# An attention layer on one core: the identity made on GpSimd, the third token tile's squares shared, eight extra weight buffers, and six changes of order

## The chip, the cores and the metric

The kernel runs on one core of a Trainium2 chip. The metric is the device time of one execution in microseconds, as the median of three runs. The engines are named as in the profile: PE is TensorE (PEld its weight loads), DVE VectorE, ACT ScalarE, POOL GpSimd, SP the engine that issues most DMAs. Each engine works through a list of its own in order, and waits for others through semaphores.

## The reference, cut to what matters

One layer over 512 tokens of width 1024, in float32:

```python
xn   = rms_norm(x, norm_gain)
proj = xn @ w_in                 # q_a k_a v_a g_a | q_i k_i w_i | c_q c_kv k_rope g_b
# group A: an indexer picks, for each query, the 128 best of the keys it may see
score = sum_h w_i[h] * relu(rope(q_i)[h] . rope(k_i)) / sqrt(512)
keys  = top_k(where(admissible, score, -1e30), 128)
o_a   = softmax(rope(norm(q_a)) . rope(norm(k_a))[keys] / 8) @ v_a[keys]
# group B: attention over latents
q_b, (k_nope, v_b) = norm(c_q) @ w_uq, norm(c_kv) @ w_ukv
o_b   = chunk_causal_softmax(norm(q_b) . norm([k_nope, k_rope]) / sqrt(96)) @ v_b
out   = x + concat(o_a * silu(g_a), o_b * silu(g_b)) @ w_out
```

Both groups have eight heads of 64. Query t may read key s if s < (t // 64 + 1) * 64.

## The kernel before, in words

Every operand of a large product is split into a high part, rounded to PE's fast float32 form, and a low part, the difference. A product of two such operands is three matmuls (`mm3`: high by high, high by low, low by high). Weights come in pieces of 128 rows by up to 512 columns: `chunk` loads a piece into a `wst` buffer (DMA issued by SP), ACT copies it to `wh` (the high part), and POOL or DVE subtracts to get `wl` (the low part).

**The opening.** The 512 tokens come as four tiles of 128 (`xin`). For each tile the squares of the first half of the columns are summed on ACT (`SQ`), those of the second half on DVE (`TTR`, a custom instruction that multiplies and sums); for tile 2 ACT takes all 1024 columns (into the buffer `big`). POOL adds the two sums and raises them to the power -0.5 (`POW`), DVE (tile 3: POOL) scales the tile by it (`SCL`), PE transposes it with the help of the identity `ident` (`x_turn`), ACT takes the high part (`XA`) and DVE the low part (`XD`) of each of 16 pieces (two halves of the tokens, eight blocks of columns). Small products with the columns for `k_i`, `w_i` and `k_rope` (`small_step`, high part `SWA`, low part `SWD`) and the products for the indexer's queries (`q_i`) follow. The order of the opening on ACT, DVE and POOL is written out by hand in three calls of `chain`.

**The middle.** `use_qi` turns the indexer's queries by their positions: two multiplications and a sum on DVE, then PE transposes them. `use_small` makes the indexer's key, whose parts are `KIH` (ACT) and `KIL` (DVE). `index` computes scores, and `topk` removes eight maxima at a time from each of three tiles (`MAX8`, `MATCH_REPLACE8`, on DVE, 16 rounds), until 128 are found; then `masks` are made from the scores (L620). Meanwhile PE runs group B's projections and attention and the projections q_a, k_a, v_a (`proj`: in `use`, the sum L905 is the last reader of the PSUM bank for k_a).

**Attention.** For each head h, `qk(h, t)` makes scores of query tile t (PE), adds the mask and takes the row minimum of the negated scores (a custom instruction on DVE, L758), and exponentiates (ACT, L760). `pt(h, b)` transposes the result in three blocks and splits it in parts (`SP[h, b]`: ACT the high part, DVE the low part `pl`, L449). `pv(h, part)` multiplies with the values, adds the two halves (L822), and for every second head multiplies with the gate (L825) and splits the result into `mah` (ACT, L827) and `mal` (L828). In group A the gate and `mal` are POOL's, save for the last pair of heads, which is DVE's. Output products start beside the last heads (`out_part`, the additions to the output `ob` on DVE, L1008).

**What sets the order.** PE's order is that of the code, which weaves several generators by hand. On the other engines a list scheduler of the framework orders the instructions. `after(v, u)` tells it to put v behind u; on one engine that adds no semaphore. `after` is the means of most edits below. Tiles of one tag share a ring of buffers (`BUFS`): a new tile waits for the last use of the one that it replaces. The first eight hardware DMAs go out freely; each later one waits for the landing of the eighth before it.

Of the kernel before, what the change touches and what calls it, by code (L numbers as in the profile page):

```python
# [11 lines left out]
AF = mybir.ActivationFunctionType  # L12
# [76 lines left out]
def layer(ctx: ExitStack, tc: tile.TileContext, x, norm_gain, w_in, a_q_norm, a_k_norm, b_q_latent,  # L89
# [121 lines left out]
    for t in range(NT):  # L211
        nc.sync.dma_start(xin[t // 2][:, t % 2], xv[:, t])
        if t == 1:
            nc.sync.dma_start(ident, cst[:, 768:896])
    for a in range(0, 8, 4):
        ks = slice(a, a + 4)
        nc.sync.dma_start(wst[:, ks, 0:32], wv[:, ks, 3272:3304])
        nc.sync.dma_start(wst[:, ks, 32:104], wv[:, ks, 2560:2632])

    nhalf = P.tile([128, 8], F32, name="nhalf")  # L220
    nc.gpsimd.memset(nhalf, -0.5)
# [67 lines left out]
    def chunk(w, k, c, n, eng, he):  # L289
        st = sb("wst", (128, n))  # L290
        nc.sync.dma_start(st, w[k * 128:(k + 1) * 128, c:c + n])
        h = sb("wh", (128, n), F32R)
        l = sb("wl", (128, n), F32R)
        if he == "A":
            copies.append(nc.scalar.copy(h, st))  # L295
        else:
            E(he).tensor_copy(h, st)
        i = E(eng).tensor_tensor(l, st, f32(h), op=OP.subtract)  # L298
        (subs if eng == "P" else dsubs).append(i)
        return h, l  # L300
# [66 lines left out]
    SQ, TTR, POW, SCL = {}, {}, {}, {}  # L367
    big = sb("qk8", (128, D), name="big")
    for t in range(NT):
        xt = xin[t // 2][:, t % 2]  # L370
        r = small(4)
        if t == 2:
            SQ[t] = nc.scalar.activation(big, xt, AF.Square, scale=D ** -0.5, accum_out=r[:, 0:1])
            other = epsc
        else:
            sq = tmp(), tmp()
            SQ[t] = nc.scalar.activation(sq[0], xt[:, 0:512], AF.Square, scale=D ** -0.5, accum_out=r[:, 0:1])
            TTR[t] = nc.vector.tensor_tensor_reduce(sq[1], xt[:, 512:], xt[:, 512:], 1.0 / D, EPS, OP.mult, OP.add, r[:, 1:2])
            other = r[:, 1:2]
        POW[t] = nc.gpsimd.tensor_tensor(r[:, 2:3], r[:, 0:1], other, op=OP.add), rsqrt(r[:, 3:4], r[:, 2:3])  # L380
        SCL[t] = []
        for xs in (xt[:, 0:512], xt[:, 512:]) if t in (0, 3) else (xt,):
            e = nc.gpsimd if t == 3 else nc.vector
            if t == 3:
                SCL[t].append(e.tensor_scalar(xs, xs, r[:, 3:4], 0.0, op0=OP.mult, op1=OP.add))
            else:
                SCL[t].append(e.tensor_scalar(xs, xs, r[:, 3:4], None, op0=OP.mult))
# [66 lines left out]
    KIL = sb("z3", (128, S), F32R, "kil")  # L454

    def use_small(_, a):
        st = tmp()
        first(nc.scalar.copy(st[:104], a[:104]), KEEP_SMALL)

        def turn():  # L460
# [18 lines left out]
            def turn2():  # L479
                p = psum("tr")  # L480
                for t in range(NT):
                    transpose(p[:, tok(t)], kid[:, t], ident)
                split(KIH, KIL, p)
            later(LAG_KI, turn2)
# [41 lines left out]
    for a in range(0, 8, 4):  # L526
        ks = slice(a, a + 4)
        SWA.append(nc.scalar.copy(SWH[:, ks], wst[:, ks]))
    for k in range(4):
# [8 lines left out]
    for i, ks in enumerate(((0,), (1,), (2, 3), (4, 5), (6, 7))):  # L538
# [3 lines left out]
        if i == 0:  # L542
            xa, xd = [[f[hf, k] for hf in range(2) for k in range(8)] for f in (XA, XD)]
            chain(wake_, SQ[0], SQ[1], SQ[2], gains_, SQ[3], *xa[:2], SWA[0], *xa[2:4], SWA[1], *xa[4:8], copies[0],
                  *xa[8:10], copies[1], *xa[10:12], copies[2], *xa[12:], copies[3], copies[4])
            chain(TTR[0], TTR[1], *SCL[0], *SCL[1], TTR[3], *SCL[2], *xd, dsubs[0], *SWD)
            chain(*POW[0], *POW[1], *POW[2], *POW[3], *SCL[3], *subs[:3])
        if i == 2:
# [15 lines left out]
    def use_qi(t, a):  # L564
# [5 lines left out]
        rope_mul(a3[:, :, 0:32], m, a3[:, :, 0:32], cs32, t, 8, 32)  # L570
        nc.vector.tensor_tensor(q3[:, :, 0:32], a3[:, :, 0:32], m, op=OP.add)

# [20 lines left out]
    def index():  # L593
        for t in (3, 2, 1):
            n = (t + 1) * 128
            acc = masks[t] = ACC[t]
            for h in range(8):
# [11 lines left out]
                yield 1  # L609

    def topk():
        for _ in range(TOPK // 8):
            for t in (3, 2, 1):
                with tc.issue_after(dve[0]):
                    m = sb("m8", (128, 8))
                    nc.vector.max(m, masks[t])  # L616
                    dve[0] = nc.vector.match_replace(masks[t], m, masks[t], -3e38).ins  # L617
                yield 1
# [126 lines left out]
    def attention(heads, turn, score, mask, nq, V, gate, finish):  # L745
# [4 lines left out]
        def qk(h, t):  # L750
# [17 lines left out]
            elif not turn and h > 1 and t == 3:  # L768
                after(m, SP[h - 2, 0][1])
            if not turn and h and t == 0:  # L770
                after(e, SP[h - 1, 0][0])
# [16 lines left out]
        def pt(h, b):  # L788
# [9 lines left out]
            if not turn and b == 2:  # L798
                for v, u in zip(SP[h, 2], SP[h, 0]):
                    after(v, u)  # L800
            PT[h, b] = ph, pl

# [3 lines left out]
        def pv(h, part):  # L806
# [14 lines left out]
            nc.scalar.copy(ov[d], o[s])  # L821
            nc.vector.tensor_tensor(ov[d], o[d], ov[d], op=OP.add)  # L822
            if h % 2:
# [3 lines left out]
                nc.scalar.copy(mh, ov)  # L827
                eng.tensor_tensor(ml, ov, f32(mh), op=OP.subtract)  # L828

# [46 lines left out]

    MB = {}

# [14 lines left out]
    def proj(name, tab):  # L893
        def use(t, a):
# [9 lines left out]
            rsqrt(r[:, 8:16], r[:, 0:8])  # L904
            (nc.gpsimd if name == "q_a" else nc.vector).tensor_tensor(q, c, m, op=OP.add)  # L905
            if name == "q_a":
# [95 lines left out]
    def out_part(name, nk, mh, ml, last=False):  # L1002
        jobs = []

        def job(c, t, a, n):
            def use(t, p):
                o = OB[c][:, t, a:a + n]
                nc.vector.tensor_tensor(o, p[:, :n], o, op=OP.add)  # L1008
                load()
# [41 lines left out]
```

## Time and profile before

| | us |
|---|---|
| median of 3 runs (lowest, highest) | 340.25 (340.21, 340.5) |
| the profiled execution | 339.3 |
| its span, first to last instruction | 337.5 |
| PE busy | 328.1 (97%) |
| DVE busy | 259.0 (77%) |
| ACT busy | 216.2 (64%) |
| POOL busy | 184.5 (55%) |

The span is what the trace covers; 1.8 us of the profiled execution lie outside it. An engine that is busy for nearly all of the span leaves few gaps, and these can be looked at one by one: in a row of the timeline the number in square brackets is the idle time of that engine just before the instruction, and behind the arrow stands what ended it. The ends of matmuls are modelled, and neighbours overlap in the rows, so the distance of two starts tells more about PE than a duration. The granted clock is 1.00 for the whole span.

### The profile page before, as it was taken

The page shows a single profiled execution, that of the slowest core. Times are in us where ns is not written, and L with a number is a line of the kernel's source. Part 1 is how long each engine was busy: PE and PEld are TensorE (multiplying, and loading weights), DVE is VectorE, ACT ScalarE, POOL GpSimd, SP SyncE. Part 2 cuts the span into 40 slices and gives each one's busy share as a digit, 9 for nine tenths or more (in the row PEclk, how much of TensorE's full clock was granted, in tenths as well). Part 3 has the DMA queues.
Part 4 walks back from the last instruction along what each step waited for, and adds up shares of the span by engine and source line. Part 5 has one row for each costly group of instructions (what it writes and reads, how often), then busy time and mean ns, then how long its engine had stood idle before and what let it go on. Part 6 is the DMA issues. An engine that isn't in the chain of part 4 may idle for free.

```text
span 337.5 us, 5484 instructions
## 1 busy us (share of the span) xinstructions
PE 328.1 (97%) x1691; PEld 273.8 (81%) x1691; DVE 259.0 (77%) x627; ACT 216.2 (64%) x531; POOL 184.5 (55%) x201
## 2 busy tenths in 40 slices
PE   7799999999999999999999999999999999999995
PEld 5688788888898988888888888888778788887884
DVE  4753779669999595778898989777997767876466
ACT  4935559583666676878877898434426988977210
POOL 2755553267899996135714579537724544747100
PEclk9999999999999999999999999999999999999999
DMA  7752443233133324014200354208966314420006
GB/s 259 206 163 72 128 119 117 62 102 95 33 103 93 93 72 148 1 34 124 69 27 1 86 139 136 78 0 204 233 157 228 108 55 140 126 63 1 2 0 249
DMA packets 28807, 34.83 MB, mean 103 GB/s; under 512 B 5341, under 2 KB 16874, under 8 KB 28778
## 3 DMA queue, kind: packets, MB, share of 16 engines
q1 hardware_dynamic: 26000, 32.52, 34.2%
q10 hardware_dynamic: 2778, 1.97, 2.1%
q8 instruction: 13, 0.21, 0.2%
q14 instruction: 16, 0.13, 0.1%
HBM read 27.14 MB, written 2.10 MB: 87 GB/s over the span
## 4 chain that ended last, share of the span: by engine, by line
PE 74%; DVE 10%; DMA 5%; issue 4%; ACT 4%; POOL 2%; SPq 1%; DVEq 0%; POOLq 0%
PE mm L130 40%; PE sc L130 11%; PE pv L130 10%; PE tr L134 5%; PE tr L130 5%; DMA wst<-in_w_in 3%; DMA xin<-in_x 2%; DVE ob L1008 2%; PE mm L134 2%; DVE acc L617 1%; DVE z L758 1%; DVE m L616 1%; ACT xh L403 1%; POOL sml L226 1%; POOL wl L298 1%
## 5 line engine op out<-in xcount | busy, mean ns | idle before, releaser
L298 POOL TENSOR_TENSOR wl<-wst,wh 128x512 fp32r<-128x512 f32 (+2 forms) x80 | 100.5, 1266 | 50.8 <-ACT wh L295 46.4
L295 ACT CAST wh<-wst 128x512 fp32r<-128x512 f32 (+2 forms) x89 | 51.1, 585 | 25.9 <-DMA wst<-in_w_in 13.8
L130 PE MATMUL mm<-wh,xh 128*128 128x512 f32 x112 | 47.1, 420 | 0.4 <-DVE tmp L905 0.4
L130 PE MATMUL mm<-wl,xh 128*128 128x512 f32 x112 | 44.5, 397 | 0.0
L130 PE MATMUL mm<-wh,xl 128*128 128x512 f32 x112 | 44.3, 395 | 0.0
L760 ACT ACTIVATE z<-z,sml 128x256 f32<-128x256 f32 (+2 forms) x64 | 35.9, 561 | 10.0 <-DVE sml L758 9.2
L784 POOL TENSOR_SCALAR z<-z,sml 128x512 f32<-128x512 f32 (+2 forms) x32 | 17.9, 560 | 42.1 <-DVE sml L780 31.4
L226 POOL TENSOR_TENSOR sml<-sml,nhalf 128x4 f32<-128x4 f32 (+2 forms) x28 | 32.5, 1163 | 14.9 <-ACT sml L903 13.7
L130 PE MATMUL mm<-xh,wh 128*128 128x512 f32 x88 | 36.7, 417 | 0.0
L130 PE MATMUL mm<-xl,wh 128*128 128x512 f32 x88 | 34.7, 395 | 0.0
L130 PE MATMUL mm<-xh,wl 128*128 128x512 f32 x88 | 34.7, 394 | 0.0
L616 DVE MAX8 m<-acc 128x8 f32<-128x512 f32 (+2 forms) x48 | 26.3, 550 | 0.0
L617 DVE MATCH_REPLACE8 acc<-m,acc 128x512 f32<-128x512 f32 (+2 forms) x48 | 25.9, 540 | 0.0
L130 PEld LDWEIGHTS mm<-wh,xl 128*128 128x128 f32 x112 | 21.1, 188 | 4.8
L130 PEld LDWEIGHTS mm<-wl,xh 128*128 128x128 f32 x112 | 21.2, 189 | 3.5 <-POOL wl L298 0.3
L130 PEld LDWEIGHTS mm<-wh,xh 128*128 128x128 f32 x112 | 21.1, 189 | 3.6 <-issue 0.8
L449 DVE TENSOR_TENSOR pl<-tr,ph 128x512 fp32r<-128x512 f32 (+1 forms) x32 | 17.6, 550 | 5.7 <-ACT ph L449 5.5
L449 ACT CAST ph<-tr 128x512 fp32r<-128x512 f32 (+1 forms) x32 | 15.1, 473 | 9.1 <-PE tr L134 8.8
L758 DVE CUSTOM_DVE_ANT_0 z<-sc,wide,nqb 128x512 f32<-128x512 f32 (+3 forms) x32 | 17.3, 542 | 4.2 <-PE sc L130 4.0
L130 PE MATMUL sc<-kl,bhl 96*128 96x512 f32 (+3 forms) x96 | 20.0, 320 | 0.0
L130 PEld LDWEIGHTS mm<-xh,wl 128*128 128x128 f32 x88 | 16.5, 188 | 4.1
L130 PEld LDWEIGHTS sc<-kl,bhl 96*128 96x128 f32 x96 | 16.6, 189 | 3.0
(248 smaller groups left out, 876.7 us busy)
## 6 DMA issues: line engine op xcount, KB each, us to landing
wst<-in_w_in SPq DMA_DIRECT2D x48, 256.0 KB, 2.7
wst<-in_w_out SPq DMA_DIRECT2D x16, 256.0 KB, 3.1
xin<-in_x SPq DMA_DIRECT2D x4, 512.0 KB, 5.1
ob<-in_x SPq DMA_DIRECT2D x8, 256.0 KB, 4.1
wst<-in_w_in SPq DMA_DIRECT2D x8, 192.0 KB, 2.4
wst<-in_w_uq SPq DMA_DIRECT2D x6, 192.0 KB, 2.4
wst<-in_w_in SPq DMA_DIRECT2D x8, 128.0 KB, 2.2
wst<-in_w_ukv SPq DMA_DIRECT2D x4, 256.0 KB, 2.9
```

Source lines behind the costliest of these rows:

```text
L130: nc.tensor.matmul(o, l, r, start=start, stop=stop)
L134: nc.tensor.transpose(o, i, idn)
L226: return nc.gpsimd.tensor_tensor(dst, src, nhalf[:, :src.shape[-1]], op=OP.pow)
L295: copies.append(nc.scalar.copy(h, st))
L298: i = E(eng).tensor_tensor(l, st, f32(h), op=OP.subtract)
L449: return nc.scalar.copy(h, p), nc.vector.tensor_tensor(l, p, f32(h), op=OP.subtract)
L616: nc.vector.max(m, masks[t])
L617: dve[0] = nc.vector.match_replace(masks[t], m, masks[t], -3e38).ins
L758: m = nc.vector.tensor_tensor_reduce(z, sc[:, :n], mask(t), nq(h, t), 3e38, OP.add, OP.min, r[:, i:i + 1])
L760: e = nc.scalar.activation(z, z, AF.Exp, bias=r[:, i:i + 1], scale=-1.0, accum_out=r[:, 2 + i:3 + i])
L784: nc.gpsimd.tensor_scalar(z, z, w, 0.0, op0=OP.mult, op1=OP.add)
L1008: nc.vector.tensor_tensor(o, p[:, :n], o, op=OP.add)
```

## The change

Parts of the opening: `ident` is no longer loaded from the constants; POOL fills it with ones and keeps the diagonal (`affine_select`). Tile 2's squares are shared between ACT and DVE as those of the other tiles; the buffer `big` goes. In the chains, tile 3's square on ACT moves behind the first two `XA`, the first `XD` on DVE moves ahead of the scaling of tile 2, and the second half of `SWA` goes from ACT to POOL, behind the scaling of tile 3. The first eight pieces of weights are loaded into buffers of another tag (`gm`), which are not needed until later; so no load among the first eleven waits for a buffer.

Orders on DVE: `KIL` gives way to the sum of the last indexer query (`QSUM[2]`), the 41st match-replace (`MR[40]`) to the sum of the last tile of k_a, and in group A's heads 6 and 7 the scores' instructions wait for the low part of block 2 of head 4, for head 4's L822, and for the ends of head 6; the first addition of `oa` waits for the low part of head 6's block 2. The low part of the third pair of heads (`mal`, h = 5) goes from POOL to DVE.

```diff
@@ layer, loads of the opening
     for t in range(NT):
         nc.sync.dma_start(xin[t // 2][:, t % 2], xv[:, t])
-        if t == 1:
-            nc.sync.dma_start(ident, cst[:, 768:896])
...
+    nc.gpsimd.memset(ident, 1.0)
+    nc.gpsimd.affine_select(ident, ident, pattern=[[-1, 128]], compare_op=OP.is_equal, fill=0.0, base=0, channel_multiplier=1)
@@ chunk
-        st = sb("wst", (128, n))
+        st = sb("gm" if len(done) < 8 else "wst", (128, n), name="wst")
@@ squares
-        if t == 2:
-            SQ[t] = nc.scalar.activation(big, xt, AF.Square, scale=D ** -0.5, accum_out=r[:, 0:1])
-            other = epsc
-        else:
-            sq = tmp(), tmp()
...
+        sq = tmp(), tmp()
+        SQ[t] = nc.scalar.activation(sq[0], xt[:, 0:512], AF.Square, scale=D ** -0.5, accum_out=r[:, 0:1])
+        TTR[t] = nc.vector.tensor_tensor_reduce(sq[1], xt[:, 512:], xt[:, 512:], 1.0 / D, EPS, OP.mult, OP.add, r[:, 1:2])
@@ use_small, turn2
-                split(KIH, KIL, p)
+                kil = split(KIH, KIL, p)[1]
+                if len(QSUM) == 3:
+                    after(kil, QSUM[2])
@@ SWA and the chains
-        SWA.append(nc.scalar.copy(SWH[:, ks], wst[:, ks]))
+        SWA.append((nc.gpsimd.tensor_copy if a else nc.scalar.copy)(SWH[:, ks], wst[:, ks]))
...
-            chain(wake_, SQ[0], SQ[1], SQ[2], gains_, SQ[3], *xa[:2], SWA[0], *xa[2:4], SWA[1], *xa[4:8], copies[0],
+            chain(wake_, SQ[0], SQ[1], SQ[2], gains_, *xa[:2], SQ[3], SWA[0], *xa[2:8], copies[0],
...
-            chain(TTR[0], TTR[1], *SCL[0], *SCL[1], TTR[3], *SCL[2], *xd, dsubs[0], *SWD)
-            chain(*POW[0], *POW[1], *POW[2], *POW[3], *SCL[3], *subs[:3])
+            chain(TTR[0], TTR[1], *SCL[0], *SCL[1], TTR[2], TTR[3], xd[0], *SCL[2], *xd[1:], dsubs[0], *SWD)
+            chain(*POW[0], *POW[1], *POW[2], *POW[3], *SCL[3], SWA[1], *subs[:3])
@@ proj, use
+            if name == "k_a" and t == NT - 1:
+                after(MR[MR_KEY], sum_)
@@ attention, qk
+                if h == 7:
+                    for v, u in zip((m, e), END[6]):
+                        after(v, u)
+            elif not turn and h == 6 and t in (1, 2):
+                after(m, SP[h - 2, 2][1] if t == 2 else OV[h - 2, 1])
@@ attention, pt and out_part
+                if h == 6:
+                    ADD["pl"] = SP[h, 2][1]
+                    if ("oa", 0, 0) in ADD:
+                        after(ADD["oa", 0, 0], ADD["pl"])
@@ attention, pv
-                eng.tensor_tensor(ml, ov, f32(mh), op=OP.subtract)
+                (nc.vector if h == 5 else eng).tensor_tensor(ml, ov, f32(mh), op=OP.subtract)
```

What this makes of the order is shown at three places on DVE. First the opening, from tile 1's scaling on. `xin_63` holds tiles 0 and 1, `xin_64` tiles 2 and 3; the instructions that write `sml` are the `TTR`, those that scale `xin` the `SCL`, and `xl` are the `XD`. Before:

```order
L387 TENSOR_SCALAR xin_63<-xin_63,sml 128x1024
L378 ISA tmp,sml<-xin_64 128x512
L378 ISA sml 128x1
L387 TENSOR_SCALAR xin_64<-xin_64,sml 128x1024
L406 SCALAR_TENSOR_TENSOR xl_105<-mm,gains,xh_103 128x256 x4
```

And of the change:

```order
L383 TENSOR_SCALAR xin_63<-xin_63,sml 128x1024
L375 ISA tmp,sml<-xin_64 128x512
L375 ISA sml 128x1
L375 ISA tmp,sml<-xin_64 128x512
L375 ISA sml 128x1
L402 SCALAR_TENSOR_TENSOR xl_106<-mm,gains,xh_104 128x256
L383 TENSOR_SCALAR xin_64<-xin_64,sml 128x1024
L402 SCALAR_TENSOR_TENSOR xl_106<-mm,gains,xh_104 128x256 x3
```

Between the scaling of tile 1 and that of tile 2 stand now two `TTR` and one `XD` instead of one `TTR`.

Second the last indexer query, before; the first row and the third and fourth are its two multiplications and its sum, which PE's next transposes read:

```order
L443 TENSOR_TENSOR tmp<-pv,cs_139 128x256
L449 TENSOR_TENSOR kil<-tr,kih 128x512
L446 TENSOR_TENSOR pv<-pv,cs_139 128x8x32
L571 TENSOR_TENSOR tmp<-pv,tmp 128x8x32
L582 TENSOR_TENSOR qi_383<-sc,qi_383 64x4x128
```

And of the change:

```order
L439 TENSOR_TENSOR tmp<-pv,cs_142 128x256
L442 TENSOR_TENSOR pv<-pv,cs_142 128x8x32
L571 TENSOR_TENSOR tmp<-pv,tmp 128x8x32
L445 TENSOR_TENSOR kil<-tr,kih 128x512
L582 TENSOR_TENSOR qi_386<-sc,qi_386 64x4x128
```

`KIL` has gone from the second to the fourth place. The 41st match-replace moves in the same manner behind the second multiplication and the sum of k_a's last tile.

Third the end of group A, as a piece before, from head 7's scores of query tile 1 on (`tmp<-pv,tmp` is head 5's L822):

```order
L758 ISA z_3835,sml<-sc,acc_506,nqa 128x256
L758 ISA sml 128x1
L780 RECIPROCAL sml<-sml 128x2
L822 TENSOR_TENSOR tmp<-pv,tmp 64x512
L1008 TENSOR_TENSOR ob<-mm,ob 128x512
L449 TENSOR_TENSOR pl<-tr,ph 128x512
L449 TENSOR_TENSOR pl<-mm,ph 128x512
L758 ISA z_3878,sml<-sc,wide,nqa 128x128
L758 ISA sml 128x1
L780 RECIPROCAL sml<-sml 128x2
```

And of the change:

```order
L762 ISA z_3838,sml<-sc,acc_509,nqa 128x256
L762 ISA sml 128x1
L789 RECIPROCAL sml<-sml 128x2
L1023 TENSOR_TENSOR ob<-mm,ob 128x512
L835 TENSOR_TENSOR tmp<-pv,tmp 64x512
L445 TENSOR_TENSOR pl<-tr,ph 128x512
L445 TENSOR_TENSOR pl<-mm,ph 128x512
L762 ISA z_3881,sml<-sc,wide,nqa 128x128
L762 ISA sml 128x1
L841 TENSOR_TENSOR mal<-tmp,mah 128x512
L789 RECIPROCAL sml<-sml 128x2
```

The new `mal` stands ahead of a reciprocal, and head 5's L822 has changed places with an addition to `ob`. A little earlier the low part of head 4's block 2 has moved ahead of head 6's scores of query tile 2.

## Rows read from the trace of the kernel before

**Rows 1.** The page, its first part: busy us of each engine, share, instructions.

```profile
PE 328.1 (97%) x1691; PEld 273.8 (81%) x1691; DVE 259.0 (77%) x627; ACT 216.2 (64%) x531; POOL 184.5 (55%) x201
```

**Rows 2.** Timeline of the opening: start, us, engine, line, out<-in, [idle before <-releaser].

```profile
5.09 0.19 POOL L380 TENSOR_TENSOR sml<-sml 128x1 f32<-128x1 f32 x1 [4.22 <-ACT tmp L377]
...
7.54 0.75 DVE L387 TENSOR_SCALAR xin<-xin,sml 128x1024 f32<-128x1024 f32 x1 [0.45 <-POOL sml L226]
...
9.07 0.19 POOL L380 TENSOR_TENSOR sml<-sml,epsc 128x1 f32<-128x1 f32 x1 [1.57 <-ACT gains L514]
...
9.22 0.69 DVE L378 CUSTOM_DVE_ANT_0 tmp<-xin 128x512 f32<-128x512 f32 x1 [0.93 <-DMA xin<-in_x]
...
10.34 0.75 DVE L387 TENSOR_SCALAR xin<-xin,sml 128x1024 f32<-128x1024 f32 x1 [0.42 <-POOL sml L226]
...
11.01 1.73 DVE L406 SCALAR_TENSOR_TENSOR xl<-mm,gains,xh 128x256 fp32r<-128x256 f32 x4
...
11.15 0.66 PE L134 MATMUL tr<-ident,xin 128*128 128x128 f32 x4 [1.71 <-DVE xin L387]
...
11.59 1.37 POOL L385 TENSOR_SCALAR xin<-xin,sml 128x512 f32<-128x512 f32 x2
...
14.95 0.28 PE L130 MATMUL mm<-xh,swh 128*104 128x256 f32 x1
15.01 0.88 DVE L406 SCALAR_TENSOR_TENSOR xl<-tr,gains,xh 128x256 fp32r<-128x256 f32 x2 [0.31 <-ACT xh L403]
...
15.55 0.36 PE L130 MATMUL mm<-xl,swh 128*104 128x256 f32 x1 [0.32 <-DVE xl L406]
```

**Rows 3.** Timeline, SP and DVE: the issue and the first use of `cs32`.

```profile
10.00 0.43 SPq L549 DMA_DIRECT2D cs<-cst  x1
...
29.87 0.29 DVE L473 TENSOR_TENSOR tmp<-tr,cs 128x128 f32<-128x128 f32 x1 [1.03 <-ACT tmp L471]
```

**Rows 4.** Timeline around the last indexer query, DVE and PE.

```profile
39.46 0.69 DVE L449 TENSOR_TENSOR kil<-tr,kih 128x512 fp32r<-128x512 f32 x1
...
40.40 0.39 PE L130 MATMUL mm<-xh,wl 128*128 128x512 f32 x1
41.10 0.63 PE L134 MATMUL sc<-ident,tmp 128*128 128x128 f32 x4 [0.31 <-DVE tmp L571]
```

**Rows 5.** Timeline around the last tile of k_a, PE and DVE.

```profile
241.39 0.54 DVE L617 MATCH_REPLACE8 acc<-m,acc 128x384 f32<-128x384 f32 x1
...
242.40 0.39 PE L130 MATMUL mm<-wl,xh 128*128 128x512 f32 x1
242.63 0.40 PE L130 MATMUL mm<-wh,xl 128*128 128x512 f32 x1
243.41 0.47 PE L130 MATMUL mm<-wh,xh 128*128 128x512 f32 x1 [0.38 <-DVE tmp L905]
```

**Rows 6.** Timeline of the masks, DVE and POOL; and a line of PE's waits.

```profile
252.70 2.85 DVE L620 TENSOR_SCALAR acc<-acc 128x512 f32<-128x512 f32 x2
...
252.61 2.73 POOL L298 TENSOR_TENSOR wl<-wst,wh 128x512 fp32r<-128x512 f32 x2
...
PE sc L130 <- DVE sml L758: 0.2, 1, 0.2
```

**Rows 7.** Timeline at the values of head 4, PE.

```profile
296.45 0.28 PE L130 MATMUL pv<-ph,va 128*128 128x256 f32 x1
...
296.96 0.38 PE L130 MATMUL pv<-pl,va 128*128 128x256 f32 x1 [0.23 <-DVE pl L449]
```

**Rows 8.** Timeline at the third pair's low part; a group of lines: `mal` on DVE.

```profile
309.40 1.28 POOL L828 TENSOR_TENSOR mal<-tmp,mah 128x512 fp32r<-128x512 f32 x1
...
309.90 0.40 PE L130 MATMUL mm<-wl,mah 128*128 128x512 f32 x1
...
310.73 0.50 PE L130 MATMUL mm<-wh,mal 128*128 128x512 f32 x1 [0.44 <-POOL mal L828]
...
L828 DVE TENSOR_TENSOR mal<-tmp,mah x1: 693/693/693, 326.6 to 326.6; 128x512 fp32r<-128x512 f32 x1
```

More of the change, by code (lines that the diff above doesn't have):

```diff
@@ L367, in layer @@
     SQ, TTR, POW, SCL = {}, {}, {}, {}
-    big = sb("qk8", (128, D), name="big")
     for t in range(NT):
@@ L371, in layer @@
         r = small(4)
-        if t == 2:
-            SQ[t] = nc.scalar.activation(big, xt, AF.Square, scale=D ** -0.5, accum_out=r[:, 0:1])
-            other = epsc
-        else:
-            sq = tmp(), tmp()
[L377 to L380, printed above, removed]
+        sq = tmp(), tmp()
+        SQ[t] = nc.scalar.activation(sq[0], xt[:, 0:512], AF.Square, scale=D ** -0.5, accum_out=r[:, 0:1])
+        TTR[t] = nc.vector.tensor_tensor_reduce(sq[1], xt[:, 512:], xt[:, 512:], 1.0 / D, EPS, OP.mult, OP.add, r[:, 1:2])
+        POW[t] = nc.gpsimd.tensor_tensor(r[:, 2:3], r[:, 0:1], r[:, 1:2], op=OP.add), rsqrt(r[:, 3:4], r[:, 2:3])
         SCL[t] = []
@@ L454, in layer @@
     KIL = sb("z3", (128, S), F32R, "kil")
+    QSUM = []
     def use_small(_, a):
@@ L570, in use_qi @@
         rope_mul(a3[:, :, 0:32], m, a3[:, :, 0:32], cs32, t, 8, 32)
-        nc.vector.tensor_tensor(q3[:, :, 0:32], a3[:, :, 0:32], m, op=OP.add)
+        QSUM.append(nc.vector.tensor_tensor(q3[:, :, 0:32], a3[:, :, 0:32], m, op=OP.add))
         def turn():
@@ L609, in index @@
                 yield 1
+    MR, MR_KEY = [], 40
     def topk():
@@ L616, in topk @@
                     nc.vector.max(m, masks[t])
-                    dve[0] = nc.vector.match_replace(masks[t], m, masks[t], -3e38).ins
+                    MR.append(nc.vector.match_replace(masks[t], m, masks[t], -3e38))
+                    dve[0] = MR[-1].ins
                 yield 1
@@ L821, in pv @@
             nc.scalar.copy(ov[d], o[s])
-            nc.vector.tensor_tensor(ov[d], o[d], ov[d], op=OP.add)
+            OV[h, 1] = nc.vector.tensor_tensor(ov[d], o[d], ov[d], op=OP.add)
             if h % 2:
@@ L875, in score_b @@
         mm3(o, qh[:, tok(t % 2)], ql[:, tok(t % 2)], kh[:, :n], kl[:, :n], True, True)
-    MB = {}
+    MB, ADD = {}, {}
     def finish_b(p):
@@ L904, in use @@
             rsqrt(r[:, 8:16], r[:, 0:8])
-            (nc.gpsimd if name == "q_a" else nc.vector).tensor_tensor(q, c, m, op=OP.add)
+            sum_ = (nc.gpsimd if name == "q_a" else nc.vector).tensor_tensor(q, c, m, op=OP.add)
+            if name == "k_a" and t == NT - 1:
+                after(MR[MR_KEY], sum_)
             if name == "q_a":
@@ L1007, in use @@
                 o = OB[c][:, t, a:a + n]
-                nc.vector.tensor_tensor(o, p[:, :n], o, op=OP.add)
+                ADD[name, c, t] = nc.vector.tensor_tensor(o, p[:, :n], o, op=OP.add)
+                if (name, c, t) == ("oa", 0, 0) and "pl" in ADD:
+                    after(ADD[name, c, t], ADD["pl"])
                 load()
```

## Prediction

> **What bounds the kernel now.** I read the page first: PE is busy for 97% of the span [rows 1]. So the span is PE's own work and a handful of gaps, and an edit on another engine counts by the gap of PE that it closes or opens, and by nothing else. PE's list of waits came second; it has nine lines, and five of them name what an edit touches: `xl`, the indexer query's sum L571, k_a's sum L905, the low part `pl`, and `mal`. Third came the timeline at each of these five.
>
> I price a gap by the distance of two starts, less the regular distance of two such matmuls. In the projections that is 242.63 - 242.40 = 0.23 for 512 columns [rows 5]; I take half of it, 0.12, for 256 columns. So the gaps are: opening 15.55 - 14.95 - 0.12 = 0.48 [rows 2]; indexer query 41.10 - 40.40 - 0.23 = 0.47 [rows 4]; k_a 243.41 - 242.63 - 0.23 = 0.55 [rows 5]; values of head 4 296.96 - 296.45 - 0.12 = 0.39 [rows 7]; third pair 310.73 - 309.90 - 0.23 = 0.60 [rows 8]. Together 2.49 us. The reader is to see that the whole case is about these, and about the new gaps that closing them may open.
>
> **The opening.** PE waits 1.71 us at 11.15 for tile 2's scaling, and DVE's scaling at 10.34 waits for POOL's power, whose first step began at 9.07 [rows 2]. The shared squares put a `TTR` on DVE in front of that step. DVE ends tile 1's scaling at 7.54 + 0.75 = 8.29, and a `TTR` takes 0.69 and 0.08 for its second instruction, so it ends at 9.06: POOL starts when it did, and ACT's shorter half ends no later than the whole did. So the long wait stays. It grows a little: two `TTR` and an `XD` stand ahead of the scaling now, and end at 9.06 + 0.77 + 0.43 (an `XD`, 1.73 for four) = 10.3 if none waits for ACT; I take 0.1 of delay.
>
> What is won is the next gap. At 14.95 PE wants the `xl` that DVE makes from 15.01 on, and DVE had waited there for ACT [rows 2]. Of DVE's sixteen `XD` one is done before the scaling, and ACT is rid of half of `SWA`; I give that the time of one `XD`, 0.43 (1.73 for four), since both are passes over a few hundred columns. So the awaited `xl` is ready at 15.45 - 0.43 = 15.0, and PE wants it at 14.95 + 0.12 + 0.1 = 15.2: the 0.48 go, less the 0.1, **0.4**.
>
> The half of `SWA` that POOL takes stands behind tile 3's scaling, 11.59 + 1.37 = 12.96 [rows 2]. The trace has no copy on POOL. Nearest below is that scaling with one input, 0.69 for 512 columns; above, a subtraction with two inputs, 1.28 [rows 8]; the half has 416 columns, so 0.56 to 1.04, ending at 13.5 to 14.0. PE's fifth small product wants it at about 13.9: the fifth to eighth products of the first half, eight matmuls of 0.12 to 0.14, end where the one at 14.95 begins, so they begin at about 13.8, and 0.1 later now. I take the lower end, since a copy has one input. At the upper, with tile 3's square and so its scaling 0.2 late as well (that square has moved behind two `XA`), PE loses 0.3 there in place of the gain; the best is 0.6, if the 0.1 doesn't come and the wait at 11.15 shrinks by as much.
>
> The identity on POOL is costed at nothing: POOL has nothing to do for 4.22 us before 5.09 [rows 2]. What it costs if that cover is too short is a rival. The buffers too: no wait of PE's for a weight stands among the nine, and the load of `cs32`, which must now queue on SP behind loads that start later or earlier, was issued at 10.00 and is first used at 29.87 [rows 3]; several us late it is still in time.
>
> **Three orders on DVE.** `KIL`, 0.69 long, stood ahead of the last query's sum [rows 4]. It steps aside, the sum comes up to 0.69 earlier, and the gap of 0.47 closes (0.4 at least, should the second multiplication wait for something). `KIL`'s readers, the scores of the index, follow later, behind these transposes: **0.47**. The 41st match-replace, 0.54 long, stood ahead of k_a's sum [rows 5]; the sum comes 0.54 earlier, the gap of 0.55 closes: **0.55**. At 296.96 PE waits for the low part that stood behind head 6's scores of tile 2; it is made first now: **0.39**, at least 0.3. Those scores come about 0.4 later, and ACT's exponential behind them is not yet due to PE.
>
> **`mal` on DVE.** POOL's took 1.28 from 309.40, behind a subtraction for a weight, while PE wanted it at 309.90 + 0.23 = 310.13 [rows 8]. On DVE one took 0.69 with POOL quiet. Beside POOL a DVE instruction can take much longer: two L620 took 2.85 beside POOL's two subtractions of 2.73 [rows 6], 1.4 each. And head 5's L822 has changed places with an addition, so POOL's gate and the high part come some 0.7 later, and `mal` meets POOL's subtraction. If it begins at 309.1 and takes 1.3, it ends at 310.4 against 310.13: 0.2 to 0.3 of the 0.60 stay. I take **0.39**, between 0.1 (a full collision and a late gate) and 0.6.
>
> **The sum.** 0.38 + 0.47 + 0.55 + 0.39 + 0.39 = 2.2 us. The profiled execution took 339.3 (span 337.5 and 1.8 around it), so 337.1 with a span of 335.3; the median stands 0.95 above it: 340.25 - 2.2 = **338.1**. With all the lower ends, k_a's at nothing (below), it is -0.3 + 0.4 + 0 + 0.3 + 0.1 = 0.5, or 339.75. With all the upper, 0.6 + 0.47 + 0.55 + 0.39 + 0.6 = 2.6, or 337.6.
>
> **The rivals.** *Handed back at the masks.* After 243 DVE has no pause to speak of until head 0's scores, and there PE waits for L758 once, 0.2 us [rows 6]. If DVE's work sets that point, PE comes 0.55 earlier and waits 0.55 longer: the gain is nothing, 338.65. For it speaks that DVE does the same work in another order. Against it, that two L620 took 2.85, as long as POOL's subtractions beside them, and ended with them [rows 6]; those subtractions need ACT's copies into buffers that PE's products free, so this stretch of DVE moves with PE. Chance 0.2.
>
> *The opening gives nothing or loses.* `SWA` late on POOL, as above: 0.4 to 0.7 less, 338.5 to 338.8. Chance 0.1.
>
> *More than forecast.* The wait at the masks goes too (0.2 to 0.4) and `mal` is in time (0.2): 337.5 to 336.9. Chance 0.07.
>
> *On the other side: the identity is late.* The place is POOL's start, where memset and `affine_select` stand ahead of the first sum of squares' halves. POOL is free from 5.09 - 4.22 = 0.87 on [rows 2]. The trace has no `affine_select`; each us by which it ends after 5.09 moves the first power and all that follows on PE by up to that. The gain of 2.2 is used up when it ends at 7.3, and the kernel is slower by over 0.2% from 8.0 on. Should it take one and a half times the free 4.22 us, it ends at 7.2 (340.2); twice, at 9.3 (342.3). Against it: for 128 columns POOL's nearest instructions take far less, 1.28 for four times the columns [rows 8], and its first sum after the pause took 0.19, with no sign of a start-up [rows 2]. Chance 0.08.
> [...]
>
> **How the numbers follow.** The forecast as summed has a chance of 0.55, with a range of its own from 337.4 to 338.6; the rest as given. 338.1 is its time. The range 337.2 to 339.4 leaves out the late identity, the outer part of *more*, and a mishap of several lower ends: about 0.15. About 0.2%, 0.68 us, is what a measurement of this kernel tells from no change: faster is below 339.57. All cases but the identity's lie there, save a tail of the lower ends: faster 0.87, same 0.08, slower 0.05.
>
> **What would show it.** In the changed kernel's list of PE's waits the lines of L571, L905 and `pl` L449 are gone and `mal`'s is about 0.2. `x_turn` of tile 2 starts still at 11.1 to 11.3; the `xl` wait behind it is gone. The matmuls of the last query's transposes start at about 40.2; each later place is earlier by the sum so far. At the masks the wait for L758 stays at 0.2 (right) or grows to 0.7 (handed back), and the L620 end with POOL's subtractions. POOL's first sum still begins at 5.1. Wrong would be: that sum late; a wait for `swh` behind 13.9; a new line in the list after 296, where head 6's scores and the addition to `ob` are later than they were.

## The result and the profile after

The changed kernel took 337.1 us (median of four executions, 336.87 to 337.65), against 340.28 (340.21 to 340.5) of the kernel before: a ratio of 0.9908, interval 0.9891 to 0.9925. It is faster, as forecast, but by 3.2 us where 2.2 were forecast, and 0.1 us below the range. The profiled execution took 337.1 with a span of 335.4; the forecast for that execution had been 337.1 and 335.3.

The page of the changed kernel, its first part (before: [rows 1]), and the whole list of PE's waits:

```profile
PE 327.5 (98%) x1691; PEld 274.0 (82%) x1691; DVE 261.3 (78%) x630; ACT 214.8 (64%) x530; POOL 183.7 (55%) x203
```
```profile
PE tr L134 <- DVE xin L383: 1.8, 1, 1.8
PE tr L130 <- DVE zero L243: 1.5, 1, 1.5
PE sc L134 <- DMA grow<-in_b_kv_latent_norm: 0.3, 1, 0.3
PE sc L130 <- DVE sml L762: 0.2, 1, 0.2
```

Of the nine lines before, the five that the edits aimed at are gone. The wait at the masks (L762) is what it was [rows 6]; the one for `grow` is new, and lies ahead of the long pause. The opening in the timeline of the changed kernel, which answers to [rows 2]:

```profile
1.11 0.29 POOL L220 TENSOR_SCALAR_AFFINE_SELECT ident<-ident 128x128 f32<-128x128 f32 x1
4.97 0.19 POOL L376 TENSOR_TENSOR sml<-sml 128x1 f32<-128x1 f32 x1 [3.56 <-ACT tmp L374]
...
9.62 0.69 DVE L375 CUSTOM_DVE_ANT_0 tmp<-xin 128x512 f32<-128x512 f32 x1 [0.49 <-DMA xin<-in_x]
...
10.64 0.74 DVE L383 TENSOR_SCALAR xin<-xin,sml 128x1024 f32<-128x1024 f32 x1
...
11.44 0.66 PE L134 MATMUL tr<-ident,xin 128*128 128x128 f32 x4 [1.84 <-DVE xin L383]
...
13.48 0.53 POOL L528 CAST swh<-smw 128x416 fp32r<-128x416 f32 x1
...
15.24 0.28 PE L130 MATMUL mm<-xl,swh 128*104 128x256 f32 x1
15.36 0.39 PE L130 MATMUL mm<-wh,xh 128*128 128x512 f32 x1
```

The `affine_select` of the identity takes 0.29 us on POOL and is done at 1.40, with no start-up to be seen, and POOL's first sum begins at 4.97; so nothing came of the late identity. The copy on POOL takes 0.53, just under the lower bound of 0.56. In this execution tile 2's scaling stands behind tile 3's `TTR`, which waits for its DMA; so it is 0.3 late, not 0.1. The later places, which answer to [rows 4, 5, 7, 8]:

```profile
39.92 0.40 PE L130 MATMUL mm<-xh,wl 128*128 128x512 f32 x1
40.15 0.60 PE L134 MATMUL sc<-ident,tmp 128*128 128x128 f32 x4
...
241.29 0.69 DVE L918 TENSOR_TENSOR tmp<-mm,tmp 128x512 f32<-128x512 f32 x1
...
241.97 0.40 PE L130 MATMUL mm<-wh,xl 128*128 128x512 f32 x1
242.21 0.39 PE L130 MATMUL mm<-wh,xh 128*128 128x512 f32 x1
...
295.19 0.28 PE L130 MATMUL pv<-ph,va 128*128 128x256 f32 x1
295.31 0.28 PE L130 MATMUL pv<-pl,va 128*128 128x256 f32 x1
...
307.39 1.11 DVE L841 TENSOR_TENSOR mal<-tmp,mah 128x512 fp32r<-128x512 f32 x1 [0.48 <-ACT mah L840]
...
308.05 0.40 PE L130 MATMUL mm<-wl,mah 128*128 128x512 f32 x1
308.56 0.50 PE L130 MATMUL mm<-wh,mal 128*128 128x512 f32 x1
```

Each pair of starts is at its regular distance now, but the last, which keeps 0.51 - 0.23 = 0.28 of its 0.60. So the two profiled executions differ by the 2.2 us of the working (339.3 - 337.1). What the working missed lies between the profiled execution of the kernel before (339.3) and the other executions (340.2 to 340.5).

### The profile page after: what moved, and what is told of

Same layout as the page of the kernel before. It is cut to its first block, busy times and chain, and to the rows that moved or that the text cites. A ratio compares the mean times of both kernels' runs of the same rounds, so it can differ in the third digit from the quotient of the medians.

```text
span 335.4 us, 5485 instructions
## 1 busy us (share of the span) xinstructions
PE 327.5 (98%) x1691; PEld 274.0 (82%) x1691; DVE 261.3 (78%) x630; ACT 214.8 (64%) x530; POOL 183.7 (55%) x203
## 4 chain that ended last, share of the span: by engine, by line
PE 91%; DVE 3%; DMA 2%; issue 1%; ACT 1%; POOL 1%; SPq 0%; DVEq 0%; POOLq 0%
PE mm L130 53%; PE sc L130 12%; PE pv L130 11%; PE tr L134 6%; PE tr L130 5%; DMA xin<-in_x 2%; PE mm L134 2%; DVE ob L1023 2%; PE sc L134 1%; PE pv L134 1%; POOL tmp L838 0%; SPq L212 0%; DVE mal L841 0%; DVE z L762 0%; DVE xin L383 0%
## 5 line engine op out<-in xcount | busy, mean ns | idle before, releaser
L300 POOL TENSOR_TENSOR wl<-wst,wh 128x512 fp32r<-128x512 f32 (+2 forms) x80 | 100.6, 1267 | 47.8 <-ACT wh L297 38.6
L227 POOL TENSOR_TENSOR sml<-sml,nhalf 128x4 f32<-128x4 f32 (+2 forms) x28 | 31.8, 1141 | 14.9 <-ACT sml L916 13.7
L762 DVE CUSTOM_DVE_ANT_0 z<-sc,wide,nqb 128x512 f32<-128x512 f32 (+3 forms) x32 | 17.3, 542 | 4.3 <-PE sc L130 4.0
```

Source lines behind the costliest of these rows:

```text
L227: return nc.gpsimd.tensor_tensor(dst, src, nhalf[:, :src.shape[-1]], op=OP.pow)
L762: m = nc.vector.tensor_tensor_reduce(z, sc[:, :n], mask(t), nq(h, t), 3e38, OP.add, OP.min, r[:, i:i + 1])
```

## The experiments

Beside each timed kernel the kernel before ran on the same chip. The executions proved to fall into two groups by their mean granted clock, the clock of PE averaged over the span. So the times are given for the executions at 0.997 and more ("full clock") and for those at 0.990 to 0.995 ("low clock"). In the profiles of four full-clock executions (changed kernel, `e1`, `e2`, `e3`; means of 0.999 to 1.000) every stretch up to 320 is at 1.00, and what the mean lacks is missing behind it. In the changed kernel's profile it is in the last us, where PE has nothing left to do: PE's last product begins at 331.36, and the clock is 0.77 from 334.4 to the end at 335.4.

### What the executions are

The kernel before again, and the changed kernel twice again, without an edit.

> The kernel before, unchanged, to see the spread of its executions and a second profile. The timed executions stand 0.95 us above the one profiled execution (339.3), and the changed kernel's profile (337.1) does not differ from its other executions. Theory 'lost in the opening': a typical execution of the kernel before loses about 0.95 us more before 16 us, where its DMAs land at times that vary; expected 340.2 to 340.5 for nearly all executions, and a profile of one of them shows PE's first matmul of the projections at about 16.7 in place of 15.75, with equal distances after it. Rival 'in the middle': the 0.95 us lie behind 16 us, at one of the waits that the orders touch. Rival 'clock': the granted clock is lower (0.997 in place of 1.000) and no single place shows it. Rival 'profiler': a profiled execution of this kernel is always faster, so the new profile gives 339.3 again.

> The changed kernel once more, unchanged. The executions of the kernel before fall into two groups: mean granted clock 0.998 to 1.000 with 338.85 to 339.84 us, and 0.992 to 0.995 with 340.1 to 340.9. Theory 'same gain in each group, the anchor was wrong': at a clock of 0.998 and more, median 337.1, which is 2.2 to 2.4 below the same group of the kernel before; some executions at 0.992 to 0.995 exist here too, at 338.3 to 338.9. Rival 'the change also rids the kernel of the low-clock executions': none of 6 to 12 below 0.997.

> The changed kernel once more. Of its 16 executions so far 3 had a granted clock below 0.997, of the kernel before 27 of 73, of the kernel with the old order at the end 7 of 11. Theory 'the share of low-clock executions has nothing to do with the edits and varies from call to call': a share anywhere between 0 and 0.6 here, the full-clock group again at 336.7 to 337.2, the low group 1.1 to 1.4 above it. Rival 'the change makes them rare': at most 2 of 12.

| | full clock: number, median, range | low clock: number, median, range |
|---|---|---|
| before, all calls | 58: 339.32 (338.85 to 340.63) | 37: 340.54 (340.08 to 340.89) |
| changed, all calls | 18: 336.93 (336.36 to 338.2) | 4: 338.64 (338.31 to 340.86) |

The rival "clock" was right that the clock differs, but a single place shows it, as the next section finds. Of the kernel before, two in five executions had a clock of 0.992 to 0.995, and they took 1.2 us more; the new profile, at 0.999, gave 338.85. The share differs by call (2 of 15 in one, 6 of 11 in another), and both groups stand on each of the three chips that ran it. The changed kernel has such executions too (4 of 22), 1.7 us above its others. At the full clock the change is worth 339.32 - 336.93 = **2.4 us**, at the low clock, by four executions, 340.54 - 338.64 = 1.9.

The four executions of the kernel before in the first comparison lie between 340.21 and 340.5; so late are most of the low-clock group and one of the 58 others (340.63). Their clocks were not recorded, so that they belong to the low group is concluded from their times, and not shown. The four of the changed kernel had 0.998 to 1.000. So the 3.2 us compare, in all likelihood, one group with the other.

### Where the clock falls

PE's longest pause in the profiles of the first comparison (1.71 us before [rows 2], 1.84 after) stands ahead of tile 2's transposes. Two kernels fill it (the changed one, `e6`, `e14`, and the one before, `e7`), one lengthens it (`e8`, of the kernel before).

```diff
     x_turn(1)
+    fill = psum("tr")
+    for _ in range(6):
+        matmul(fill, zero[:, 0:128].bitcast(F32R), zero.bitcast(F32R), True, True)
     x_turn(2)
```
```diff
+    sl = tmp()
+    SLOW = [nc.vector.memset(sl, 0.0) for _ in range(3)]
...
-            chain(TTR[0], TTR[1], *SCL[0], *SCL[1], TTR[3], *SCL[2], *xd, dsubs[0], *SWD)
+            chain(TTR[0], TTR[1], *SCL[0], *SCL[1], TTR[3], *SLOW, *SCL[2], *xd, dsubs[0], *SWD)
```

> The changed kernel with six products of zeros on PE between the transposes of tile 1 and of tile 2, where PE waits 1.8 us: about 1.4 us of work that nothing reads, in a pause that it does not lengthen. Theory 'the low-clock executions come from that pause': all executions at 0.997 and more, median 337.0 to 337.2. Rival 'they come from elsewhere': a share of 0.992 to 0.995 as in the other kernels. Rival 'the fill is in the way': 337.3 or more at the full clock, the transposes of tile 2 later than 11.5.

> The same six products of zeros in the kernel before. Theory 'the low-clock executions come from the pause': none below 0.997, median 339.4. Rival 'from elsewhere': about 4 of 10 executions below 0.997, as in the kernel before, median 339.5 to 340.

> The kernel before with three memsets of 128x512 on DVE (each 0.48 us by itself) ahead of the scaling of tile 2, so that PE's pause before 11.15 is about 0.9 us longer. Theory 'the low-clock executions come from the pause': nearly all executions below 0.997 and a time of 339.4 + 0.9 + 1.2 = 341.5, and the profile shows a granted clock below 1 behind the pause. Rival 'from elsewhere': 340.3 at the full clock, and the usual share of low-clock executions.

> The changed kernel with six products of zeros in PE's pause before tile 2's transposes, again. None of 18 executions of filled kernels was below 0.997. Theory 'the pause is the cause': none here either, median 336.9 to 337.2, and not above the changed kernel's full-clock group. Rival 'those 18 were luck': 2 or more of 6 to 12 below 0.997.

Filled, none of 12 changed and none of 12 of the kernel before ran below 0.997 (medians 336.94 and 339.32, as the full-clock groups without a fill). With the longer pause (2.99 us in the profile) all four did, at clocks of 0.990 to 0.995, 341.54. The stretches of that last kernel (length, busy time of PE, PEld, DVE, ACT and POOL, then PE's granted clock, DMA share, GB/s):

```profile
10.00:12.00 2.00, 0.00 (x0) 0.00 (x0) 1.65 (x4) 2.00 (x6) 1.82 (x5) 1.00 1.04 335
12.00:14.00 2.00, 1.53 (x7) 1.53 (x8) 2.00 (x6) 2.00 (x6) 0.97 (x1) 0.51 0.82 282
14.00:16.00 2.00, 2.00 (x14) 2.00 (x13) 1.55 (x4) 0.23 (x1) 1.29 (x1) 0.64 0.20 50
16.00:18.00 2.00, 2.00 (x19) 1.98 (x17) 0.88 (x2) 1.85 (x5) 0.42 (x1) 1.00 0.34 103
```

PE does nothing from 10 to 12, and then runs at half the clock (0.51 from 12 to 14; the 0.64 from 14 to 16 puts its end at about 15.4). The time of 341.5 was forecast, but not its parts: tile 2's transposes start at 12.47, 1.4 later than on average without the memsets (0.9 was expected), and the low clock behind them costs 0.7 here (1.2 was expected). That the same happens without a lengthened pause is shown by the kernel `e12` below, whose profiled execution had a clock of 0.993. Its stretches, and PE's rows there:

```profile
10.00:12.00 2.00, 0.82 (x5) 0.82 (x6) 1.92 (x7) 1.95 (x7) 1.51 (x3) 0.87 0.96 319
12.00:14.00 2.00, 2.00 (x12) 2.00 (x11) 2.00 (x6) 1.52 (x4) 1.86 (x4) 0.50 0.96 304
14.00:16.00 2.00, 2.00 (x16) 2.00 (x16) 0.10 (x2) 0.93 (x3) 0.88 (x1) 0.78 1.01 362
16.00:18.00 2.00, 2.00 (x15) 1.80 (x14) 1.63 (x4) 2.00 (x6) 1.51 (x2) 1.00 1.07 382
```
```profile
11.18 0.87 PE L134 MATMUL tr<-ident,xin 128*128 128x128 f32 x4 [1.90 <-DVE xin L383]
...
13.13 0.41 PE L130 MATMUL mm<-xh,swh 128*104 128x256 f32 x1
13.34 0.41 PE L130 MATMUL mm<-xl,swh 128*104 128x256 f32 x1
...
15.64 0.28 PE L130 MATMUL mm<-xl,swh 128*104 128x256 f32 x1
15.76 0.28 PE L130 MATMUL mm<-xh,swh 128*104 128x256 f32 x1
```

The products of 256 columns start 0.21 apart at half the clock and 0.12 apart behind it. In the changed kernel's profile nearly the same pause (1.84) was followed by a clock of 1.00, and so was a longer one in the profile of `e4`, the next section's kernel:

```profile
11.31 0.66 PE L134 MATMUL tr<-ident,xin 128*128 128x128 f32 x4 [2.18 <-DVE xin L383]
```
```profile
12.00:14.00 2.00, 2.00 (x21) 2.00 (x19) 2.00 (x6) 1.94 (x6) 1.97 (x4) 1.00 0.94 313
```

So the low clock came only where the pause stood unfilled, but its length alone does not decide (1.84 and 2.18 without the fall, 1.90 with it); what does stays open.

The same fall costs the two kernels differently. PE's first products of the projections in `e12` and in `e8`:

```profile
16.70 0.39 PE L130 MATMUL mm<-wh,xh 128*128 128x512 f32 x1
```
```profile
17.79 0.39 PE L130 MATMUL mm<-wh,xh 128*128 128x512 f32 x1
```

In `e12`, with the new opening, this product begins 16.70 - 11.18 = 5.52 behind tile 2's transposes in place of 3.92: 1.6 lost. In `e8`, with the old one, it is 17.79 - 12.47 = 5.32 in place of 4.60: 0.7, and the wait for `xl` is missing from its list, presumably since the slower products (0.21 apart) leave DVE the time. That may be why the low group is only 1.2 above the other before, but 1.7 after the change.

### The two halves of the change, and the identity

`e2`: the identity is a DMA again. `e3`: the whole opening is as before. `e4`: only the opening is changed.

```diff
+        if t == 1:
+            nc.sync.dma_start(ident, cst[:, 768:896])
...
-    nc.gpsimd.memset(ident, 1.0)
-    nc.gpsimd.affine_select(ident, ident, pattern=[[-1, 128]], compare_op=OP.is_equal, fill=0.0, base=0, channel_multiplier=1)
```

> The changed kernel with the identity loaded by a DMA between the token tiles again; everything else as changed. Theory 'lost in the opening', by the identity's DMA among the token tiles: 337.9 to 338.1 (0.8 to 1.0 lost). Rival (the identity's load is hidden, as the prediction had it, which costed its removal at nothing): 337.1, within 0.2.

> The changed kernel with its opening undone (identity by DMA, tile 2's square on ACT alone, chains and SWA as before, weights' buffers as before): only the orders on DVE and mal are new. By the two profiles these are worth 0.47 + 0.54 + 0.5 + 0.33 less 0.2 at 56 to 58 us, so about 1.7. Theory 'lost in the opening': the 0.95 stay, 340.28 - 1.7 = 338.5. Rival 'in the middle': 337.6.

> The kernel before with the changed opening alone; the orders on DVE and mal are as before. Theory 'lost in the opening': 340.28 - 0.39 - 0.95 = 338.9. Rival 'in the middle': 339.9. If the parts add up, the gains of this kernel and of the one with the orders alone sum to 3.2.

At full clock: `e2` 336.8 (4 executions; 2 more at low clock), so the identity's place is worth nothing that shows, as forecast; `e3` 337.89 (5; 1 low), so the opening is worth 0.96; `e4` 338.44 (11; 1 low), so it is worth 339.32 - 338.44 = 0.88 and the orders 338.44 - 336.93 = 1.51. The two halves add up to the whole within 0.1. The times expected for `e3` and `e4`, of theory and rival alike, were missed, since they were counted from 340.28; the theory that a load in the opening costs 0.95 fell with `e2` and with the groups above.

In the traces, PE's first product of the projections begins 4.60 behind tile 2's transposes with the old opening (15.75 - 11.15, [rows 2]) and 15.36 - 11.44 = 3.92 with the new one. Two rows of the kernel before, which stand around the gap from 14.95 to 15.55:

```profile
14.75 0.36 PE L130 MATMUL mm<-xl,swh 128*104 128x256 f32 x1
...
15.75 0.39 PE L130 MATMUL mm<-wh,xh 128*128 128x512 f32 x1
```

The difference is 0.68: the 0.48 of the gap, and 0.1 each in the distances on both sides of it, which were 0.20 in place of 0.12. The transposes themselves start at 10.7 to 11.4, moved by when the tokens land (DVE waits for their DMA 0.93 us in [rows 2], 0.49 in the changed kernel's profile), on average at 11.1 in 13 profiles with the new opening and at 11.0 in four with the old one (10.8 to 11.3). Where the 0.2 between this 0.7 and the 0.9 of the medians come from stays open.

### The orders one by one

Each of these takes one order out of the changed kernel, or, the last, one group of orders.

```diff
@@ e9
-                if len(QSUM) == 3:
-                    after(kil, QSUM[2])
@@ e10
-            if name == "k_a" and t == NT - 1:
-                after(MR[MR_KEY], sum_)
@@ e11
-                (nc.vector if h == 5 else eng).tensor_tensor(ml, ov, f32(mh), op=OP.subtract)
+                eng.tensor_tensor(ml, ov, f32(mh), op=OP.subtract)
@@ e12
-                if h == 7:
-                    for v, u in zip((m, e), END[6]):
-                        after(v, u)
-            elif not turn and h == 6 and t in (1, 2):
-                after(m, SP[h - 2, 2][1] if t == 2 else OV[h - 2, 1])
...
-                        after(ADD["oa", 0, 0], ADD["pl"])
```

> The changed kernel with KIL ahead of the last query's sum again. Executions at a granted clock of 0.997 and more are compared (changed kernel 336.98, 13 of them). Theory 'each order is worth its gap of PE': the gap before the last query's transposes is back (0.47), and the lags of the index's scores at 54 to 58 us (0 to 0.66, which the changed kernel's profiles show in the place of that gap) go: 337.0 + 0.47 - 0.1 to 0.3 = 337.15 to 337.35. Rival 'no net gain, KIL only moves the wait': 336.9 to 337.0.

> The changed kernel with the 41st match-replace ahead of k_a's sum again. Theory 'the gain stays, as DVE's stretch at the masks moves with PE': the gap at k_a is 0.55 to 0.8 in place of 0.1 to 0.36, and the wait at the masks stays at 0.38: 337.3 to 337.45 at full clock. Rival 'handed back at the masks': the gap is there, the distance at the masks (0.38) shrinks to its regular size, and the time is 337.0.

> The changed kernel with the third pair's low part on POOL again. The distance ahead of the product with it was 0.60 too long before, and is 0.27 in the changed kernel, where DVE's subtraction took 1.11 beside POOL's. Theory: with POOL's the product waits at least as long as before, since the gate is also 0.7 later now, 0.6 to 1.2: 337.3 to 337.9 at full clock. Rival 'the place is covered': 337.0.

> The changed kernel with the order on DVE in heads 6 and 7 as before (mal stays on DVE, KIL and match-replace stay as changed). Theory: the distance of 0.39 too long at head 4's values is back, and as L822 is early again mal meets less: 337.0 + 0.4 - 0 to 0.27 = 337.1 to 337.4 at full clock. Rival 'a new wait in the changed order eats the gain': 337.0 or less.

`e9`, 337.62 (five, all at full clock): 0.69 lost, more than the expected 0.15 to 0.35. The gap is back (0.46 over the regular distance):

```profile
39.61 0.40 PE L130 MATMUL mm<-xh,wl 128*128 128x512 f32 x1
40.30 0.63 PE L134 MATMUL sc<-ident,tmp 128*128 128x128 f32 x4 [0.29 <-DVE tmp L569]
```

The profiled execution (337.94) had also a wait of 0.7 that only it shows and that nothing in the profile ends; the other four are at 337.25 to 337.66, so the 0.2 beyond the gap stay open.

`e10`, 337.13 (five at full clock): 0.2 lost, between what the theory (0.3 to 0.45) and the rival (nothing) had. The gap is back, and the wait at the masks is as in the changed kernel, so nothing is handed back there. Rows of `e10`, PE:

```profile
241.51 0.40 PE L130 MATMUL mm<-wh,xl 128*128 128x512 f32 x1
242.27 0.47 PE L130 MATMUL mm<-wh,xh 128*128 128x512 f32 x1 [0.36 <-DVE tmp L918]
...
260.13 0.39 PE L130 MATMUL mm<-wh,mbl 128*128 128x512 f32 x1
260.75 0.38 PE L130 MATMUL sc<-k_a,q_a 128*128 128x256 f32 x1 [0.23 <-DVE sml L762]
```

But the order does not always close the gap. In the profiled execution of `e5`, the changed kernel again, the opening was quicker:

```profile
240.68 0.69 DVE L918 TENSOR_TENSOR tmp<-mm,tmp 128x512 f32<-128x512 f32 x1
...
240.93 0.40 PE L130 MATMUL mm<-wh,xl 128*128 128x512 f32 x1
241.52 0.47 PE L130 MATMUL mm<-wh,xh 128*128 128x512 f32 x1 [0.19 <-DVE tmp L918]
```

PE came here 241.97 - 240.93 = 1.04 earlier than in the first profile of the changed kernel, DVE's sum 241.29 - 240.68 = 0.61: the rest is waited for, 0.36 over the regular distance. In `e13` 0.24 are left, and in `e11` below, which keeps this order, 0.53:

```profile
241.63 0.40 PE L130 MATMUL mm<-wh,xl 128*128 128x512 f32 x1
242.39 0.47 PE L130 MATMUL mm<-wh,xh 128*128 128x512 f32 x1 [0.36 <-DVE tmp L918]
```

So at k_a DVE, busy with the removal of maxima, is as much the bound as PE: in `e5` PE came 1.04 earlier, and waited 0.36 there.

`e11`, 337.78 (five at full clock): 0.85 lost, more than the 0.60 that `mal` on POOL cost before. Rows of POOL and PE:

```profile
308.01 1.29 POOL L841 TENSOR_TENSOR mal<-tmp,mah 128x512 fp32r<-128x512 f32 x1
...
308.16 0.40 PE L130 MATMUL mm<-wl,mah 128*128 128x512 f32 x1
309.36 0.51 PE L130 MATMUL mm<-wh,mal 128*128 128x512 f32 x1 [0.80 <-POOL mal L841]
```

The distance ahead of the last product is 1.20, which is 0.97 too long: 0.69 more than in the changed kernel. It is more than the 0.60 before, because in the changed order head 5's L822, and with it POOL's gate, comes later: POOL's `mal` begins only 0.15 ahead of PE's product in the second row, before it was 0.50 [rows 8]. The rest of the loss may be the wait at k_a above.

`e12`: 337.06 at full clock (4 executions), 338.6 at low clock (7 of 11, the greatest share of all kernels but `e8`). At full clock only 0.1 is lost: the wait at head 4's values is back (0.38), and the one for `mal` is gone. Rows of PE:

```profile
296.46 0.28 PE L130 MATMUL pv<-ph,va 128*128 128x256 f32 x1
296.96 0.39 PE L130 MATMUL pv<-pl,va 128*128 128x256 f32 x1 [0.22 <-DVE pl L445]
...
309.92 0.40 PE L130 MATMUL mm<-wl,mah 128*128 128x512 f32 x1
310.15 0.41 PE L130 MATMUL mm<-wh,mal 128*128 128x512 f32 x1
```

So one of the orders of this group gives back most of what the order at head 4 wins; the suspect is the one that puts head 5's L822 behind an addition.

Two kernels test it: one leaves out that order alone (`e16`, the edit below), the other all orders of that group but the one at head 4's values (`e15`). Both have the fill.

```diff
-            elif not turn and h == 6 and t in (1, 2):
-                after(m, SP[h - 2, 2][1] if t == 2 else OV[h - 2, 1])
+            elif not turn and h == 6 and t == 2:
+                after(m, SP[h - 2, 2][1])
```

> The changed kernel with the fill of PE's pause, and of the orders in heads 6 and 7 only the low part of head 4 ahead of head 6's scores of query tile 2; the others are as the scheduler makes them (head 5's L822 ahead of the addition to ob again). Theory 'two orders in this group pull against each other': the low part's 0.39 stays won, and mal, 0.7 earlier, no longer makes PE wait (the 0.27 of the changed kernel go): 336.94 - 0.27 = 336.65, none below a granted clock of 0.997. Rival 'the changed place of head 4's L822 costs what mal gives back': 336.9 to 337.1.

> The same with only the order behind head 4's L822 left out of the changed ones: head 7's scores wait for head 6's end and the first addition of oa for head 6's low part as in the change. Theory as for the other: 336.65 at full clock, none below 0.997; the two do not differ beyond 0.2. Rival: 336.9 to 337.1.

Their profiles show neither wait, and from the masks (PE's first product behind L762) to the end PE takes 70.65 in both, against 70.92 in the changed kernel: 0.27, as expected. In the medians that does not show: 336.99 and 337.07 (six each, all at full clock) were expected at 336.65, and are no better than 336.93, which is what the rival said. `e16`'s profile has a wait of 0.5 ahead of the masks, for a weight's low part from POOL (L300), that the changed kernel's three profiles do not have (`e4`'s has one too). With such waits, and tile 2's transposes up to 0.7 us earlier or later (10.7 to 11.4), six executions do not resolve 0.27, so whether it is won stays open. None of these twelve executions had a low clock.

## Why the prediction was wrong

**The step that failed** is in *The sum*: "the median stands 0.95 above it: 340.25 - 2.2 = **338.1**". It carried the 0.95 between the profiled execution and the median over to the changed kernel, as something that stays, and gave no reason. What the runs show in its place is two groups of executions of one kernel: 339.32 at full clock and 340.54 at low clock before the change. The profiled execution (339.3, clock 1.00) is of the first; the executions of the median lie, by their times, with the second. The four of the changed kernel were at 0.998 to 1.000, so the forecast to compare them with was the other one in the same sentence, 337.1. Among the rivals none had a granted clock that differs between executions.

It is partly luck that this other forecast is met to the tenth, since sizes that were off nearly cancel (below). And it was chance which group the four fell into: four other executions of the changed kernel, at low clock, took 338.31 to 340.86, and a median of such ones would have stood higher by 1.7, inside the range.

**Right, by its own terms:** the identity at nothing (0.29 of POOL's free 4.2, and `e2`); the buffers at nothing, as far as the changed kernel's three profiles go, which have no wait of PE's for a weight (`e4` and `e16`, with the same buffers, have one of 0.5 each, and no run tests the buffers alone); `KIL` 0.47 (the gap is gone, and 0.46 is back in `e9`, whose median lost 0.69); the low part at head 4 0.39 (0.38 comes back in `e12`); the wait at the masks unchanged (*handed back* is out by `e10`); `SWA` on POOL at the lower end.

**Sizes that were off.** The opening, 0.38 forecast: 0.7 by the traces and 0.9 by the medians. The distances beside its gap were too long as well, which the working did not count, and of the 0.1 of delay there is 0.06 on average. The match-replace, 0.55 forecast: 0.54 in one profile, but 0.2 by the medians (`e10`), and of the gap 0.36 were left in `e5` and 0.24 in `e13`, since DVE is late there as well; the working took DVE's sum to come early enough however early PE is. The third pair, 0.39 forecast: 0.60 - 0.28 = 0.32, since DVE's subtraction beside POOL's took 1.11 and came late through the order at L822; the working had named both, but took the order's cost for a part of `mal`, while it belongs to the edit next to it. Together these errors nearly cancel: 2.4 at full clock in place of 2.2.

**Open:** why two in five executions of the kernel before had the low clock, 4 of 22 of the changed one, and 7 of 11 of `e12`. With shares that differ so much by call, nothing here shows that the change makes it rarer.

## What to carry to other kernels

Where a profiled execution is faster than every timed one, look at the granted clock of the executions before the difference is carried into a forecast: they may be two groups (here 339.32 and 340.54), and a median of few can fall into one of them. The profile of `e12` has a clock of 0.50 behind a pause of PE near the start (1.90 us), and 1.6 us lost behind it; six products of zeros in the pause cost nothing that shows (336.94 against 336.93, and 339.32 with and without them). Price a gap by the starts on both sides of it and by their neighbours, and ask of the engine that ends it whether it can be earlier at all; a gap that one profile shows closed (k_a, changed kernel) was 0.36 over its regular distance in the next (`e5`).

## What the hardware showed unexpectedly

With nearly the same program, PE's granted clock stayed at 1.00 behind a pause of 1.84 us in one execution (changed kernel), and behind one of 2.18 in another (`e4`), but stood at 0.50 from about 11.5 to 14.9 behind a pause of 1.90 in a third (`e12`). Executions with a low mean clock took 1.2 us more before the change and 1.7 more after it. Six products of zeros in the pause left none of 36 executions with a low clock (`e15` and `e16` counted), and with three memsets more on DVE ahead of it four of four had one (0.990 to 0.995). Beside a subtraction of POOL's (306.66 to 307.95), DVE's subtraction for `mal`, from 307.39 on, took 1.11, where another of this shape took 0.69 with POOL quiet [rows 8].
